# The product with w_out as seven products of halves, on a hybrid decoder block in fp32

## The chip, the cores and the metric

The kernel runs on one core of a Trainium2 chip. The metric is the device time of one execution in microseconds, as the median of several runs. Before the change it is 1438.05 us (three runs, 1435.02 to 1439.66).

## What is computed

One decoder block on 1024 tokens of width 1024, all in float32. The change concerns the second line from the end of the mixer and the layer norm behind it:

```python
proj = x @ w_in                       # q | f | i | og | pool_v | gate_a | gate_b
a = HGRN2(q, f, i) -> per-head RMSNorm * sigmoid(og) -> @ w_a
b = per-group linear(causal_mean_w(pool_v) - pool_v) * pool_scale
merged = sigmoid(gate_a) * a + sigmoid(gate_b) * b
x = layer_norm(alpha * x + merged @ w_out, ln1_g, ln1_b)
x = layer_norm(alpha * x + relu(x @ w_up)^2 @ w_down, ln2_g, ln2_b)
```

w_out is 1024 x 1024, w_up 1024 x 4096.

## The kernel before, in words

**Precision.** TensorE multiplies in a rounded fp32 form, so each operand is split into a high part (a copy in that form, on ScalarE) and a low part (operand minus high part, on VectorE). A product of two operands is three matmuls: high by high, high by low and low by high (mm3, L110 to L116).

**Seven products.** The products with w_in, w_a, w_up and w_down are computed with halves of tokens, of the contraction and of the columns by seven products instead of eight, with sums of halves made on VectorE ahead of them. The product with w_out is not: `mix(t, cc)` computes token tile t (128 tokens) by column half cc (512 columns) as 8 x 3 matmuls of 128x512 into one bank of PSUM. VectorE adds it to alpha times the row of x (L1390), takes statistics (L1332), and after the second half comes the layer norm of the row: aggregate (L1338), square root on ScalarE (L1339), normalising on ScalarE (L1350), times gamma on VectorE (L1351), plus beta on GpSimd (L1352). The rows 6 and 7 use two passes on VectorE instead (L1343, L1346), in halves of the row.

**Stages.** `a_pair(p)` makes two 128-row blocks of a, transposed (width by tokens), by seven products. `gated` loads the gate and the pooled branch from DRAM, multiplies and adds on VectorE (L1269, L1270) and gets a tile of merged: 128 of the width by 512 tokens. In before each is split at once (`split_act`, L121 and L122), or, for the first two pairs, kept in a pool and split later (`unpark`). The list `then` says what is recorded behind each of the seven steps of the last two pairs: there the rows of the first column half of w_out are loaded and split (`out_row`, L1253 and L1254). Then all `mix` calls are recorded: both halves of tiles 0 to 3, the transposes of these tokens for the MLP (`first_tokens`), and tiles 4 to 7.

**What sets the order.** The program is recorded in the order of the code, and a list scheduler with priorities (`tc.high_priority(PRIO)`) places each engine's instructions. Each engine then works its own queue strictly in order, and an instruction that waits holds up all behind it. Loads go out on SP, in its order, as soon as the buffer is free. `act_tile` gives an operand tile of two halves of 512 (high and low), `c_tile` and `block_tile` other 128x512 buffers, and `w_tile` the parts of a weight. The PSUM tags are "pj" (4 banks), and "hg", "sc" and "tr".

Of the kernel before, what the change touches and what calls it, by code (L numbers as in the profile page):

```python
# [13 lines left out]
ALU = mybir.AluOpType  # L14
# [38 lines left out]
def tile_hybrid_block(  # L53
# [119 lines left out]
    def transposed(tiles, off, kp, tag):  # L173

        ps = ps_tile(tag, 2)
        for c in range(CH):
            done = PE.transpose(ps[:, c * P : (c + 1) * P], tiles[c][:, off + kp * P : off + (kp + 1) * P], ident)
        return ps, done.ins
# [577 lines left out]
    with tc.tile_pool(name="tmp", bufs=1, side="right", reuse_waits="tile") as tmp:  # L756
# [492 lines left out]
        pk, parked, wo = [], {}, []  # L1249

        def out_row(raw, tile_of):
            hi, lo = tile_of()
            A.copy(hi, raw)  # L1253
            V.tensor_sub(lo, raw, f(hi))  # L1254
            wo.append((hi, lo))

        def parts_of(tile_of):
            def two():
                t = tile_of()
                return t[:, 0], t[:, 1]  # L1260
            return two

        def gated(j, u, park):

            def take(src):
                with tc.issue_after(last_load[0]):
                    t = loaded(gad[j][u], mg_tile("ga", 10))
# [3 lines left out]
                if park:  # L1271
                    parked[u, j] = t
                else:
                    merged[u][j] = split_act(t)
# [14 lines left out]
        def unpark(*which):  # L1289
            for u, j in which:  # L1290
                merged[u][j] = split_act(parked[u, j])

        def out_rows_of(*ks):
            for k in ks:
                out_row(loaded(w_out[k * P : (k + 1) * P, :HALF], c_tile), parts_of(act_tile))
# [17 lines left out]
    with tc.tile_pool(name="pk", bufs=1, side="right", reuse_waits="tile") as parking:  # L1313
        pk.append(parking)
        for i in range(2, 7):
            step(i)
        two = [a_pair(p) for p in range(2, 4)]
        then = (
            lambda: unpark((0, 0), (0, 1), (0, 2), (0, 3)), lambda: out_rows_of(0, 1, 2, 3), lambda: out_rows_of(4, 5, 6, 7),
            lambda: None, lambda: None, lambda: None, lambda: None,  # L1320
        )
        for i, after in enumerate(then):
            run(*(p[i : i + 1] for p in two))
            after()
        unpark((1, 0), (1, 1), (1, 2), (1, 3))
# [41 lines left out]
    xt[0] = [c_tile() for _ in range(CH)]  # L1367
    with tc.tile_pool(name="wo", bufs=1, side="right", reuse_waits="tile") as mp:
        st1 = [None] * 8
        g1, b1 = ln_params(lambda: f(act_tile()).rearrange("p a b -> p (a b)"), ln1_g, ln1_b)  # L1370
        for k2 in range(0, KT, 2):
            raw = raw_rows(w_out, k2, 1)
            for k in range(2):
                n = len(wo)
                out_row(raw[k], (
                    (lambda: (row_tile(), row_tile())) if n < 10 else
                    parts_of(act_tile if n < 12 else lambda: mp.tile([P, 2, HALF], F32R, tag="wo", name=nm("wo"), bufs=4))
                ))

        def mix(t, cc):  # L1380
            u, c = divmod(t, CH)
            if cc == 0:
# [7 lines left out]
            V.scalar_tensor_tensor(rc, rc, ALPHA, ps, ALU.mult, ALU.add)  # L1390
            stats(r[t], cc, st1[t])
            if cc == 1:
# [5 lines left out]
        for cc in range(2):  # L1398
            for t in range(CH):
                mix(t, cc)  # L1400
# [286 lines left out]
```

## Time and profile before

| | before |
|---|---|
| median of three runs | 1438.05 us |
| the profiled execution | 1434.66 us, span 1433.0 us |
| granted clock of TensorE | 0.999 |
| busy: TensorE, VectorE, ScalarE, GpSimd | 99%, 77%, 53%, 8% of the span |
| first w_out matmul, first MLP product | 710.3 us, 811.9 us |
| last w_a products | up to about 727 us, between the first w_out ones |

In the profile, PE is TensorE, DVE VectorE, ACT ScalarE and POOL GpSimd; PEld are the loads of the stationary operand. A row of a group gives the line, the engine, the operation, the tiles written and read, the shape, the count, then busy time and the mean ns of one, then the idle time before it and what ended that. A row of a timeline gives start, duration, engine, line, operation and tiles. Consecutive instructions of one engine overlap a little, so that they start closer together than they last.

### The profile page before, as it was taken

The page shows a single profiled execution, that of the slowest core. Times are in us where ns is not written, and L with a number is a line of the kernel's source. Part 1 is how long each engine was busy: PE and PEld are TensorE (multiplying, and loading weights), DVE is VectorE, ACT ScalarE, POOL GpSimd, SP SyncE. Part 2 cuts the span into 40 slices and gives each one's busy share as a digit, 9 for nine tenths or more (in the row PEclk, how much of TensorE's full clock was granted, in tenths as well). Part 3 has the DMA queues.
Part 4 walks back from the last instruction along what each step waited for, and adds up shares of the span by engine and source line. Part 5 has one row for each costly group of instructions (what it writes and reads, how often), then busy time and mean ns, then how long its engine had stood idle before and what let it go on. Part 6 is the DMA issues. An engine that isn't in the chain of part 4 may idle for free.

```text
span 1433.0 us, 21208 instructions
## 1 busy us (share of the span) xinstructions
PE 1420.8 (99%) x7499; PEld 1180.1 (82%) x7499; DVE 1099.2 (77%) x1832; ACT 753.2 (53%) x1376; POOL 110.9 (8%) x300
## 2 busy tenths in 40 slices
PE   9999999999999999999999999999999999999997
PEld 7888888888888888878888888888888888888886
DVE  6967887897797796679965697666666887777978
ACT  5445566566656656455522376555556433433534
POOL 0002011111212110100003000000000100000000
PEclk9999999999999999999999999999999999999999
DMA  7142254444444546899551315444457864444422
GB/s 272 60 140 89 90 131 148 126 115 150 113 118 133 150 123 190 237 322 340 182 198 74 103 59 188 153 159 161 162 177 243 299 235 146 150 151 157 132 74 118
DMA packets 187179, 228.18 MB, mean 159 GB/s; under 512 B 12576, under 2 KB 111168, under 8 KB 187072
## 3 DMA queue, kind: packets, MB, share of 16 engines
q1 hardware_dynamic: 180464, 210.94, 44.6%
q0 software_dynamic: 5824, 13.63, 4.7%
q10 hardware_dynamic: 784, 2.25, 0.5%
q8 instruction: 59, 0.97, 0.3%
q14 instruction: 48, 0.39, 0.1%
HBM read 149.70 MB, written 77.07 MB: 158 GB/s over the span
## 4 chain that ended last, share of the span: by engine, by line
PE 95%; DVE 2%; DMA 1%; ACT 1%; issue 1%; POOL 0%; DVEq 0%; ACTq 0%; SPq 0%; POOLq 0%
PE ps_pj L219 16%; PE ps_pj L222 16%; PE ps_pj L221 16%; PE ps_pj L1565 4%; PE ps_pj L1566 4%; PE ps_pj L1564 4%; PE ps_pj L115 2%; PE ps_pj L114 2%; PE ps_pj L116 2%; PE ps_tr L1566 2%; PE ps_tr L1565 2%; PE ps_tr L1564 2%; PE ps_hg L219 1%; PE ps_sc L219 1%; PE ps_sc L222 1%; PE ps_hg L221 1%
## 5 line engine op out<-in xcount | busy, mean ns | idle before, releaser
L219 PE MATMUL ps_pj<-act,w 128*128 128x512 f32 x1068 | 419.9, 393 | 0.3 <-ACT c L303 0.2
L222 PE MATMUL ps_pj<-act,w 128*128 128x512 f32 x1068 | 415.3, 390 | 0.0
L221 PE MATMUL ps_pj<-act,w 128*128 128x512 f32 x1068 | 415.3, 389 | 0.0
L256 ACT CAST w<-raw 128x512 fp32r<-128x512 f32 x303 | 187.7, 621 | 255.4 <-PE ps_pj L221 169.7
L257 DVE TENSOR_TENSOR w<-raw,w 128x512 fp32r<-128x512 f32 x303 | 207.2, 686 | 93.6 <-ACT w L256 92.3
L219 PEld LDWEIGHTS ps_pj<-act,w 128*128 128x128 f32 x1068 | 200.5, 188 | 44.1 <-ACT c L303 1.3
L222 PEld LDWEIGHTS ps_pj<-act,w 128*128 128x128 f32 x1068 | 200.5, 188 | 42.4
L221 PEld LDWEIGHTS ps_pj<-act,w 128*128 128x128 f32 x1068 | 200.6, 188 | 40.5
L1526 ACT CAST act<-act 128x1024 fp32r<-128x1024 f32 x66 | 67.0, 1050 | 108.2 <-issue 35.0
L1527 DVE TENSOR_TENSOR act<-act,act 128x1024 fp32r<-128x1024 f32 x66 | 79.4, 1220 | 18.1 <-ACT act L1526 18.1
L1566 PE MATMUL ps_pj<-act,act 128*128 128x512 f32 x240 | 93.0, 389 | 0.0
L1565 PE MATMUL ps_pj<-act,act 128*128 128x512 f32 x240 | 93.0, 389 | 0.0
L1564 PE MATMUL ps_pj<-act,act 128*128 128x512 f32 x240 | 92.5, 389 | 0.0
L307 DVE TENSOR_TENSOR c<-c,ps_pj 128x512 f32<-128x512 f32 x91 | 62.1, 682 | 32.5 <-PE ps_pj L222 31.8
L303 ACT COPY c<-ps_pj 128x512 f32<-128x512 f32 x92 | 53.3, 581 | 3.0 <-PE ps_pj L222 1.9
L1564 PEld LDWEIGHTS ps_pj<-act,act 128*128 128x128 f32 x240 | 45.0, 188 | 9.4
L1565 PEld LDWEIGHTS ps_pj<-act,act 128*128 128x128 f32 x240 | 45.0, 188 | 9.4
L1566 PEld LDWEIGHTS ps_pj<-act,act 128*128 128x128 f32 x240 | 45.0, 188 | 9.3
L312 DVE TENSOR_TENSOR raw<-raw,raw 128x512 f32<-128x512 f32 x43 | 29.6, 689 | 25.5 <-DMA raw<-in_w_in_dram 16.1
L1435 ACT ACTIVATE c<-c 128x512 f32<-128x512 f32 x61 | 38.5, 632 | 1.7
L1434 ACT ACTIVATE c<-c 128x512 f32<-128x512 f32 x46 | 29.0, 632 | 16.4 <-DVE c L307 16.4
L751 POOL DMA_DIRECT2D s<-og x28 | 24.9, 1161 | 133.2 <-DVE og L1177 133.2
(433 smaller groups left out, 2684.6 us busy)
## 6 DMA issues: line engine op xcount, KB each, us to landing
h<-c SPq DMA_DIRECT2D x106, 256.0 KB, 3.0
raw<-in_w_in_dram SPq DMA_DIRECT2D x100, 256.0 KB, 3.3
act<-h SPq DMA_DIRECT2D x78, 256.0 KB, 3.0
draw<-in_w_down_dram SPq DMA_DIRECT2D x16, 1024.0 KB, 8.2
raw<-in_w_up_dram SPq DMA_DIRECT2D x56, 256.0 KB, 2.9
hf<-h SPq DMA_DIRECT2D x34, 256.0 KB, 3.0
s<-og POOLq DMA_DIRECT2D x28, 256.0 KB, 6.4
v<-v SPq DMA_DIRECT2D x16, 256.0 KB, 3.5
```

The costliest lines, as they stand in the source:

```text
L219: PE.matmul(ps, wh[:, k], th, start=first and k == 0, stop=False, skip_group_check=True)
L221: PE.matmul(ps, wh[:, k], tl, start=False, stop=False, skip_group_check=True)
L222: PE.matmul(ps, wl[:, k], th, start=False, stop=k == CH - 1, skip_group_check=True)
L256: hi_of.append(A.copy(hi, src).ins)
L257: lo_of.append(V.tensor_sub(lo, src, f(hi)).ins)
L303: noted(A.copy(t, ps))
L307: last_add[0] = V.tensor_add(t, t, ps).ins
L1526: A.copy(hi, src)
L1527: V.tensor_sub(lo, src, f(hi))
L1564: PE.matmul(ps, hh[:, w], wh, start=fresh and n == 0, stop=False, skip_group_check=True)
L1565: PE.matmul(ps, hh[:, w], wl, start=False, stop=False, skip_group_check=True)
L1566: PE.matmul(ps, hl[:, w], wh, start=False, stop=n == M - 1, skip_group_check=True)
```

## The change

Tokens are halved into u = 0 (tiles 0 to 3) and u = 1, the contraction and the columns of w_out into halves as well. With A11, A12 the two halves of merged of the first tokens, A21, A22 those of the second, and B11, B12, B21, B22 the quarters of w_out, the products are p1 = A11 B11, p2 = A12 B21, p3 = S4 B22, p4 = A22 T4, p5 = S1 T1, p6 = S2 T2, p7 = S3 T3. The sums of tokens are S3 = A11 - A21 (GpSimd), S2 = A22 - S3, S1 = S2 + A11 and S4 = A12 - S2 (VectorE); those of rows are T3 = B22 - B12, T1 = B12 - B11, T2 = T3 + B11 and T4 = B21 - T2 (GpSimd). Each product is 4 token tiles by 4 row blocks by 3 terms. p6, p5 and p3 accumulate in the banks of p1, p4 in those of p7, which p2 had before; every stage of these sums is added to its row of x at once on VectorE (L1417, L1419 in the changed kernel), 28 evictions in all. On TensorE the scheduler puts the products in the order p1, half of p2's contraction, p6, p5, the rest of p2, p3, p7, transposes, p4, transposes.

The high parts of all rows and sums of rows are cast on ScalarE (L1292), their low parts made on GpSimd (L1293). The parking of gated tiles goes: those of the last two pairs are loaded into halves of operand tiles (`half_act`) and are split where they are used. The rows of tokens 0 to 3 are finished by p3, and their layer norm follows each; the transposes `first_tokens` come between p7 and p4; rows 4 to 7 are finished by p4. Layer norm itself is the same code (L1371, L1374, L1379 and L1380 are the changed kernel's lines for L1343, L1346, L1351 and L1352 of before).

```diff
-        ps = ps_tile(tag, 2)
+        ps = ps_tile(tag, 4 if tag == "pj" else 2)
...
-        pk, parked, wo = [], {}, []
-
-        def out_row(raw, tile_of):
-            hi, lo = tile_of()
-            A.copy(hi, raw)
-            V.tensor_sub(lo, raw, f(hi))
-            wo.append((hi, lo))
-
-        def parts_of(tile_of):
-            def two():
-                t = tile_of()
-                return t[:, 0], t[:, 1]
-            return two
+        pk, free_halves = [], []
+
+        def half_act():
+            if not free_halves:
+                t = f(act_tile())
+                free_halves.extend((t[:, 0], t[:, 1]))
+            return free_halves.pop(0)
...
-                    t = loaded(gad[j][u], mg_tile("ga", 10))
+                    t = merged[u][j] = loaded(gad[j][u], mg_tile("ga", 8) if park else half_act)
...
+        def split_rows(srcs, tile_of):
+            made = []
+            for t in srcs:
+                hi, lo = tile_of()
+                A.copy(hi, t)
+                G.tensor_sub(lo, t, f(hi))
+                made.append((hi, lo))
...
+        def split_a11():
+            out_ops["p1"] = [split_tokens(tokens(0, 0))]
+            for k in range(CH):
+                G.tensor_sub(merged[1][k], merged[0][k], merged[1][k])
+
+        def split_b11():
+            b_rows["b11"] = out_rows(0, 0, c_tile)
+            out_ops["p1"].append(split_rows(b_rows["b11"], act_parts))
+
+        def make_t3_t1():
+            b12, b22 = b_rows["t1"], b_rows["t3"] = [out_rows(kh, 1, half_act) for kh in range(2)]
+            for k in range(CH):
+                G.tensor_sub(b22[k], b22[k], b12[k])
+                G.tensor_sub(b12[k], b12[k], b_rows["b11"][k])
+
+        def make_t2():
+            b_rows["t2"] = b_rows["b11"]
+            for t, t3 in zip(b_rows["t2"], b_rows["t3"]):
+                G.tensor_add(t, t3, t)
+
+        def split_t2():
+            out_ops["p6"] = [split_rows(b_rows["t2"], act_parts)]
...
+    then = split_a11, lambda: None, split_b11, make_t3_t1, make_t2, split_t2, lambda: None
...
-            ps = ps_tile()
-            w = slice(c * P, (c + 1) * P)
-            mm3(ps, [(merged[u][k][0][:, w], merged[u][k][1][:, w], *wo[cc * KT + k]) for k in (0, 1, 2, 3, 4, 6, 5, 7)])
-            rc = r[t][:, cc * HALF : (cc + 1) * HALF]
-            V.scalar_tensor_tensor(rc, rc, ALPHA, ps, ALU.mult, ALU.add)
-            stats(r[t], cc, st1[t])
...
-        for cc in range(2):
-            for t in range(CH):
-                mix(t, cc)
...
+    chains = [[ps_tile(tag, 2) for tag in ("hg", "hg", "tr", "tr")], [ps_tile() for _ in range(CH)]]
...
+            for k, ((xh, xl), (wh, wl)) in enumerate(zip(xs, ws)):
+                PE.matmul(ps, xh[:, w], wh, start=fresh and k == 0, stop=False, skip_group_check=True)
+                PE.matmul(ps, xh[:, w], wl, start=False, stop=False, skip_group_check=True)
+                PE.matmul(ps, xl[:, w], wh, start=False, stop=k == CH - 1, skip_group_check=True)
+            y = r[t][:, nh * HALF : (nh + 1) * HALF]
+            with tc.high_priority(PRIO):
+                if (t, nh) in begun:
+                    V.tensor_add(y, y, ps)
+                else:
+                    V.scalar_tensor_tensor(y, y, ALPHA, ps, ALU.mult, ALU.add)
+                    begun.add((t, nh))
+                if whole:
+                    stats(r[t], nh, st1[t])
+            if then:
+                then(t)
...
+    s2 = [half_act() for _ in range(CH)]
+    for k in range(CH):
+        V.tensor_sub(s2[k], merged[1][CH + k], merged[1][k])
+    out_ops["p6"].insert(0, split_tokens(s2))
+    r = [None] * 8
+    out_product("p1", 1, True, 0, 0, False)
+    for k in range(CH):
+        V.tensor_add(merged[0][k], s2[k], merged[0][k])
+    out_ops["p5"] = split_tokens(tokens(0, 0)), split_rows(b_rows["t1"], row_parts)
+    out_product("p6", 1, False, 1, 0, False)
+    b21 = out_rows(1, 0, raw_row)
+    out_ops["p2"] = split_tokens(tokens(0, 1)), split_rows(b21, act_parts)
+    t4 = [half_act() for _ in range(CH)]
+    for t, row, t2 in zip(t4, b21, b_rows["t2"]):
+        G.tensor_sub(t, row, t2)
+    out_product("p5", 1, False, 1, 1, False)
+    for k in range(CH):
+        V.tensor_sub(merged[0][CH + k], merged[0][CH + k], s2[k])
+    out_ops["p3"] = split_tokens(tokens(0, 1)), split_rows(out_rows(1, 1, c_tile), row_parts)
+    out_product("p2", 0, True, 0, 0, True)
+    out_ops["p7"] = split_tokens(tokens(1, 0)), split_rows(b_rows["t3"], act_parts)
+    out_product("p3", 1, False, 0, 1, True, norm_row)
+    out_ops["p4"] = split_tokens(tokens(1, 1)), split_rows(t4, act_parts)
+    out_product("p7", 0, True, 1, 1, True)
+    xt[:] = [r[c][:, HALF:] for c in range(CH)], [c_tile() for _ in range(CH)], [r[c][:, :HALF] for c in range(CH)]
+    first_tokens("a12", "pj")
+    first_tokens("a11", "pj")
+    out_product("p4", 0, False, 1, 0, True, norm_row)
```

Three places of the order. The first is GpSimd around the end of the w_a products. Before, behind the last loads of o, it has nothing but the adds of beta:

```order
L735 DMA c_1373_7244<-o6_0_940 128x512
L735 DMA c_1375_7249<-o7_0_942 128x512
L1352 TENSOR_TENSOR r_1593_8246<-r_1593_8246,act_1574_8202 128x1024
L1352 TENSOR_TENSOR r_1596_8276<-r_1596_8276,act_1574_8202 128x1024
L1352 TENSOR_TENSOR r_1599_8306<-r_1599_8306,act_1574_8202 128x1024
L1352 TENSOR_TENSOR r_1602_8336<-r_1602_8336,act_1574_8202 128x1024
```

In the changed kernel the loads of o are followed by the sums T3 (L1318), T1 (L1319), T2 (L1324) and low parts of rows (L1293); c_1510 to c_1513 hold the rows of B11 and then T2, act_1522 and act_1523 B12 and then T1, act_1524 and act_1525 B22 and then T3; here its last part:

```order
L1319 TENSOR_TENSOR act_1523_7876<-act_1523_7876,c_1512_7821 128x512
L1293 TENSOR_TENSOR w_1582_8283<-act_1522_7873,w_1581_8282 128x512
L1318 TENSOR_TENSOR act_1525_7882<-act_1525_7882,act_1523_7876 128x512
L1293 TENSOR_TENSOR act_1542_7993<-c_1510_7817,act_1542_7993 128x512
L1293 TENSOR_TENSOR act_1543_7996<-c_1511_7819,act_1543_7996 128x512
L1324 TENSOR_TENSOR c_1512_7821<-act_1525_7882,c_1512_7821 128x512
L1293 TENSOR_TENSOR w_1584_8287<-act_1522_7873,w_1583_8286 128x512
L1319 TENSOR_TENSOR act_1523_7876<-act_1523_7876,c_1513_7823 128x512
L1293 TENSOR_TENSOR w_1586_8291<-act_1523_7876,w_1585_8290 128x512
L1293 TENSOR_TENSOR act_1544_7999<-c_1512_7821,act_1544_7999 128x512
L1324 TENSOR_TENSOR c_1513_7823<-act_1525_7882,c_1513_7823 128x512
L1293 TENSOR_TENSOR w_1588_8295<-act_1523_7876,w_1587_8294 128x512
```

Forty-eight instructions of 128x512 have come ahead of the adds of beta; the last T2 is the L1324 into c_1513_7823, the last row but one here.

The second place is where the last w_a product leaves its bank, which p1's last token tile takes over. ScalarE in the changed kernel: L1292 are casts of rows of w_out (c_1512 and c_1513 are T2, c_1615 is a row of B22), L121 casts of S2 (act_1563, act_1564) and of A11:

```order
L1292 CAST w_1585_8290<-act_1523_7876 128x512
L1292 CAST act_1544_7999<-c_1512_7821 128x512
L1292 CAST w_1587_8294<-act_1523_7876 128x512
L1292 CAST w_1619_8476<-c_1615_8468 128x512
L1292 CAST act_1545_8002<-c_1513_7823 128x512
L1389 DMA act_1553_8172<-in_ln1_g_dram 128x1024
L1389 DMA act_1554_8174<-in_ln1_b_dram 128x1024
L121 CAST act_1565_8190<-act_1563_8184 128x512
L121 CAST act_1566_8193<-act_1563_8184 128x512
L121 CAST act_1567_8196<-act_1564_8185 128x512
L121 CAST act_1568_8199<-act_1564_8185 128x512
```

The casts of S2 stand behind those of T2. VectorE in the changed kernel, S1's sums (L1446), the low parts of S2 (L122) and the last gated tile (L1263 reads the bank, L1264 adds the pooled branch):

```order
L1446 TENSOR_TENSOR ga_1469_7638<-act_1563_8184,ga_1469_7638 128x512
L122 TENSOR_TENSOR act_1565_8190<-act_1563_8184,act_1565_8190 128x512
L1446 TENSOR_TENSOR ga_1416_7416<-act_1564_8185,ga_1416_7416 128x512
L122 TENSOR_TENSOR act_1566_8193<-act_1563_8184,act_1566_8193 128x512
L1446 TENSOR_TENSOR ga_1471_7656<-act_1564_8185,ga_1471_7656 128x512
L122 TENSOR_TENSOR act_1567_8196<-act_1564_8185,act_1567_8196 128x512
L1263 TENSOR_TENSOR act_1550_8025<-act_1550_8025,ps_pj_1486_7698 128x512
L122 TENSOR_TENSOR act_1568_8199<-act_1564_8185,act_1568_8199 128x512
L1264 TENSOR_TENSOR act_1550_8025<-act_1550_8025,gb_1551_8027 128x512
```

and in before, with the same gated tile at L1269 and L1270:

```order
L1269 TENSOR_TENSOR ga_1559_8026<-ga_1559_8026,ps_pj_1484_7683 128x512
L1270 TENSOR_TENSOR ga_1559_8026<-ga_1559_8026,gb_1560_8028 128x512
L122 TENSOR_TENSOR act_1561_8032<-ga_1559_8026,act_1561_8032 128x512
L1269 TENSOR_TENSOR ga_1562_8047<-ga_1562_8047,ps_pj_1486_7698 128x512
L1270 TENSOR_TENSOR ga_1562_8047<-ga_1562_8047,gb_1563_8049 128x512
L122 TENSOR_TENSOR act_1564_8053<-ga_1562_8047,act_1564_8053 128x512
L122 TENSOR_TENSOR act_1565_8056<-ga_1444_7523,act_1565_8056 128x512
L122 TENSOR_TENSOR act_1566_8059<-ga_1461_7593,act_1566_8059 128x512
L122 TENSOR_TENSOR act_1567_8062<-ga_1447_7544,act_1567_8062 128x512
```

Before, the eviction (L1269 from ps_pj_1486_7698) stands behind the low parts of the tiles just ahead of it; in the change it stands behind three low parts of S2, whose casts come behind T2's.

The third place is the end of the product on VectorE. In the changed kernel (r_8298 to r_8346 are rows 4 to 7, L133 low parts of the transposes of the first tokens):

```order
L1417 TENSOR_TENSOR r_8330<-r_8330,ps_tr_8178 128x512
L1376 RECIPROCAL lmv_8857<-lmv_8857 128x1
L1417 TENSOR_TENSOR r_8346<-r_8346,ps_tr_8179 128x512
L1360 BN_STATS lst_8331<-r_8330 128x6
L1377 TENSOR_SCALAR lmv_8857<-lmv_8857 128x1
L1360 BN_STATS lst_8347<-r_8346 128x6
L133 TENSOR_TENSOR act_8789<-ps_pj_8784,act_8789 128x512
L1366 BN_AGGR lmv_8880<-lst_8331 128x2
L133 TENSOR_TENSOR act_8798<-ps_pj_8793,act_8798 128x512
L1366 BN_AGGR lmv_8903<-lst_8347 128x2
L133 TENSOR_TENSOR act_8807<-ps_pj_8802,act_8807 128x512
L1371 SCALAR_TENSOR_TENSOR r_8330<-r_8330,lmv_8880,act_8172 128x512 x2
```

In before, rows 6 and 7 (r_8714, r_8780):

```order
L1332 BN_STATS lst_8715<-r_8714 128x6
L1338 BN_AGGR lmv_8771<-lst_8715 128x2
L1343 SCALAR_TENSOR_TENSOR r_8714<-r_8714,lmv_8771,act_8200 128x512 x2
L1344 RECIPROCAL lmv_8771<-lmv_8771 128x1
L1346 SCALAR_TENSOR_TENSOR r_8714<-r_8714,lmv_8771,act_8202 128x512 x2
L1390 SCALAR_TENSOR_TENSOR r_8780<-r_8780,ps_pj_8783 128x512
L1332 BN_STATS lst_8781<-r_8780 128x6
L1390 SCALAR_TENSOR_TENSOR r_8780<-r_8780,ps_pj_8810 128x512
L1332 BN_STATS lst_8781<-r_8780 128x6
L1338 BN_AGGR lmv_8837<-lst_8781 128x2
L1343 SCALAR_TENSOR_TENSOR r_8780<-r_8780,lmv_8837,act_8200 128x512 x2
```

Before, row 6 has gone through its layer norm when row 7's first half is evicted; in the change the rows 6 and 7 are evicted one after the other, with row 5's layer norm and the transposes' low parts still in the queue.

More of the change, by code (lines that the diff above doesn't have):

```diff
@@ L1311, in tile_hybrid_block @@
             step(i)
[L1313 to L1325, printed above, removed]
+    pk_scope = ExitStack()
+    pk.append(pk_scope.enter_context(tc.tile_pool(name="pk", bufs=1, side="right", reuse_waits="tile")))
+    for i in range(2, 7):
+        step(i)
+    two = [a_pair(p) for p in range(2, 4)]
+    then = split_a11, lambda: None, split_b11, make_t3_t1, make_t2, split_t2, lambda: None
+    for i, after in enumerate(then):
+        run(*(p[i : i + 1] for p in two))
+        after()
     mg_scope.close()
@@ new lines, in raw_row, with row_parts @@
+    def raw_row():
+        return block_tile((HALF,))
+    def row_parts():
+        return row_tile(), row_tile()
+    s2 = [half_act() for _ in range(CH)]
[7 more added lines that the diff above has]
+    out_ops["p5"] = split_tokens(tokens(0, 0)), split_rows(b_rows["t1"], row_parts)
@@ L1409, in tile_hybrid_block @@
+    pk_scope.close()
     M = 4
```

64 lines of the change are left out of this document (28 added, 36 removed).

## The prediction

> **What bounds the kernel now.** I read the page first, for the busy shares and the chain that ended last, and then the waits of TensorE.
>
> ```profile
> PE 1420.8 (99%) x7499; PEld 1180.1 (82%) x7499; DVE 1099.2 (77%) x1832; ACT 753.2 (53%) x1376; POOL 110.9 (8%) x300
> PE 95%; DVE 2%; DMA 1%; ACT 1%; issue 1%; POOL 0%; DVEq 0%; ACTq 0%; SPq 0%; POOLq 0%
> PE ps_hg L480 <- POOL ident masks.py:199: 1.8, 1, 1.8
> PE ps_tr L114 <- DVE f L905: 1.4, 1, 1.4
> ```
>
> TensorE is busy for 99% of the span, the chain is TensorE for 95% of it, and its two longest waits are 1.8 and 1.4 us. A matmul that is taken away is therefore worth its whole slot, as long as nothing new makes TensorE wait. How much room the other engines have around the product with w_out is in the view by stretches of 20 us, and the slot of a matmul is in the timeline of TensorE.
>
> ```profile
> 680.00:700.00 20.00, 20.00 (x90) 16.57 (x89) 19.54 (x33) 11.48 (x21) 0.00 (x0) 1.00 0.55 170
> 700.00:720.00 20.00, 20.00 (x90) 16.57 (x89) 18.54 (x31) 8.46 (x16) 0.00 (x0) 1.00 0.58 177
> 720.00:740.00 20.00, 20.00 (x90) 16.53 (x90) 15.82 (x26) 7.08 (x13) 0.00 (x0) 1.00 0.69 254
> 740.00:760.00 20.00, 20.00 (x90) 16.57 (x89) 9.92 (x18) 5.50 (x7) 2.74 (x2) 1.00 0.36 112
> 760.00:780.00 20.00, 20.00 (x94) 16.40 (x93) 10.13 (x21) 4.79 (x8) 6.84 (x3) 1.00 0.19 79
> 800.00:820.00 20.00, 20.00 (x101) 16.92 (x100) 14.73 (x26) 5.82 (x12) 0.00 (x0) 1.00 0.32 107
> 840.00:860.00 20.00, 19.78 (x87) 16.03 (x87) 20.00 (x34) 14.77 (x27) 0.00 (x0) 1.00 0.16 53
> ```
> ```profile
> 710.30 0.39 PE L114 MATMUL ps_pj<-act,act 128*128 128x512 f32 x1
> ...
> 710.98 0.39 PE L114 MATMUL ps_pj<-act,act 128*128 128x512 f32 x1
> ...
> 785.66 1.03 PE L177 MATMUL ps_tr<-ident,r 128*128 128x128 f32 x8
> ```
>
> The columns are PE, weight loads, DVE, ACT and POOL busy, then the granted clock (1.00). VectorE is nearly full up to 720 us (19.54 and 18.54 of 20), half idle from 740 to 780, and full again at 840 to 860, where TensorE has its only small hole. GpSimd does nothing before 740. Three matmuls take 0.68 us, so one takes 0.227 us; eight transposes take 1.03 us, of which the last one's own duration is about 0.27, so one takes about 0.11 us.
>
> **What goes.** The product has 8 token tiles by 2 halves by 24 matmuls, 384; seven products of 4 tiles by 4 rows of w_out by 3 terms by 4 are 336. 48 x 0.227 = **-10.9 us** on TensorE.
>
> **What is added elsewhere.** Durations are from the groups by form between 600 and 880 us, and the spacing of queued VectorE instructions from its timeline.
>
> ```profile
> L122 DVE TENSOR_TENSOR act<-ga,act 128x512 fp32r<-128x512 f32 x16 | 10.7, 688 | 2.8 <-ACT act L121 2.7
> L121 ACT CAST act<-ga 128x512 fp32r<-128x512 f32 x16 | 9.4, 620 | 17.4 <-DVE ga L1270 17.4
> L1390 DVE SCALAR_TENSOR_TENSOR r<-r,ps_pj 128x512 f32<-128x512 f32 x16 | 10.9, 684 | 15.6 <-PE ps_pj L116 14.9 <-DMA r<-in_x_dram 0.7
> L1352 POOL TENSOR_TENSOR r<-r,act 128x1024 f32<-128x1024 f32 x6 | 14.4, 2399 | 149.0 <-DVE r L1351 137.2 <-PE ps_tr L177 9.3 <-DMA x<-r 2.5
> ```
> ```profile
> 692.82 0.69 DVE L257 TENSOR_TENSOR w<-raw,w 128x512 fp32r<-128x512 f32 x1
> 693.42 0.69 DVE L1270 TENSOR_TENSOR ga<-ga,gb 128x512 f32<-128x512 f32 x1
> 694.02 0.68 DVE L307 TENSOR_TENSOR room<-room,ps_pj 128x512 f32<-128x512 f32 x1
> ```
>
> A VectorE instruction on 128x512 starts every 0.60 us. VectorE gets 12 more evictions (28 for 16), 12 more low parts of tokens (28 for 16) and 12 sums, and loses the 16 low parts of w_out: +20, about 12 us. ScalarE gets 24 more casts, 24 x 0.62 = 15 us in a stage where it is at most 11.5 of 20 busy; I charge nothing for them by themselves: they lie in its idle time, and where one stands in a chain it is in the waits below. The gated tiles are now loaded into halves of operand tiles that TensorE frees late; the first such load goes out at 694.4 (70 matmuls ahead of the 710.3 mark) and so lands some 3 us after the place of its first use in before. VectorE has lost four low parts of w_out right behind it, 2.4 us, and I charge 0; without that cover it is 3 us. GpSimd gets 28 low parts and 20 sums, 48 instructions of 128x512. Its only large operation before is the six adds of 2.40 us for 128x1024. Half of it is 1.20 us; with a fixed part as large as a whole small operation (0.2 us, below) it would be 1.30. I take 1.20, so 48 are 58 us where there was nothing.
>
> **What the path sees of it: the first wait.** In the order of the changed kernel, p1's last token tile needs the bank that the last w_a product leaves. Its eviction (L1263 into act_1550_8025 from ps_pj, shown with the change) stands on VectorE behind the low parts of S2, their casts stand on ScalarE behind the casts of T2 (L1292), and the last of those waits for the last sum on GpSimd (L1324). So GpSimd's sums now reach TensorE. p1's last tile starts 84 matmuls after the place of the first w_out product: 710.3 + 84 x 0.227 = 729.4.
>
> Queues alone: the 18 GpSimd instructions from the first T3 to the last T2 can begin when b22 has come. Its buffers are freed 49 matmuls ahead of the 710.3 mark, at 699.2; six loads stand ahead of it on SP.
>
> ```profile
> 698.35 1.02 SPq L723 DMA_DIRECT2D c<-in_w_out_dram  x2
> ...
> raw<-in_w_in_dram SPq DMA_DIRECT2D x100, 256.0 KB, 3.3
> ```
>
> Six loads at 0.5 us and its own 3.3 make 705.5, some 706 with the wait for the buffer. 706 + 18 x 1.20 = 727.6; then one cast, and about 5 us of casts, low parts and evictions: 733.5, **4 us late**, and 2 to 3 us more where p2's rows b21 are cast and split behind it. 6.5 us in all.
>
> **A second price: VectorE and GpSimd get in each other's way.** The trace of before shows it at GpSimd's small operations.
>
> ```profile
> L1038 POOL TENSOR_TENSOR dec<-p x16: 190/198/776, 125.9 to 518.1; 128x4 f32<-128x4 f32 x16
> ```
> ```profile
> 164.90 0.68 POOL L1038 TENSOR_TENSOR dec<-p 128x4 f32<-128x4 f32 x1
> 165.52 0.18 POOL L1042 COPY eq<-p 128x4 f32<-128x4 f32 x1
> ...
> 514.95 1.49 POOL L1029 COPY T<-tA 128x32 f32<-128x32 f32 x1 [0.95 <-DVE tA L1014]
> ```
> ```profile
> 164.84 0.68 DVE L1050 TENSOR_TENSOR q<-q,tA 128x512 f32<-128x512 f32 x1
> 165.44 0.74 DVE L1116 COPY_PREDICATED att<-cmask,sc 128x512 f32<-128x512 uint32 x1
> ...
> 515.38 0.43 DVE L931 TENSOR_TENSOR pC<-pA 128x269 f32<-128x269 f32 x1
> 515.73 0.68 DVE L1018 TENSOR_TENSOR_SCAN tC<-f,starts 128x255 f32<-128x255 f32 x1
> ```
>
> L1038 has a median of 0.198 us. At 164.90 it took 0.68: VectorE had begun L1050, with two inputs in SBUF, at 164.84, and L1038 ended when that did. The next small one, beside an instruction that also reads a PSUM score, took 0.18. At 514.95 a copy of 128x32 took 1.49 us and ended with VectorE's second instruction in a row. So GpSimd stands still while VectorE reads two tiles of SBUF. The other direction, VectorE behind a long GpSimd operation, the trace cannot show: the six adds of 2.40 us met only VectorE instructions with a PSUM input, statistics and small ones.
>
> The Trainium skill, "SBUF — State Buffer", section "Who interferes with whom", says that a VectorE instruction with two SBUF inputs and a GpSimd instruction that reads SBUF exclude each other for a whole instruction, whichever starts first. The rows above agree for the one direction, and no row of before shows the other. By that rule the change pays the sum of the two queues instead of the longer one; without it, the queues alone.
>
> I take the two queues as one where both read SBUF. From the moment that L1264 ends the last gated tile of the first half of tokens (L1270 in before, 693.42, so 694.1), the rows up to p1's last bank are 23 of GpSimd and 32 of VectorE with two SBUF inputs: 23 x 1.20 + 32 x 0.60 = 46.8 us, 740.9, against the 729.4 that TensorE wants: **11.5 us late** in place of 4. On to the last low part for p3 (L1293 of c) there are 19 of GpSimd and 29 of VectorE, 22.8 + 17.4 = 40.2: 781.1, against 710.3 + 252 x 0.227 = 767.5: **13.6 us late**. That is no second stall of its size but 2 us more. The lower end is the 6.5 us of the queues alone, as if GpSimd held nobody up; the upper one 17, with 3 us more for casts and low parts that come behind the sums. The rows of GpSimd's small operations lie at the upper side: **+14**.
>
> **The end of the product.** In before the row of a token tile is finished every 24 matmuls or later; in the changed kernel rows 4 to 7 are all finished inside p4, one every 12 matmuls, 2.7 us. Their layer norms crowd together.
>
> ```profile
> L1332 DVE BATCH_NORM_STATS2 lst<-r 128x6 f32<-128x512 f32 x16 | 11.0, 692 | 0.4
> L1351 DVE TENSOR_TENSOR r<-r,act 128x1024 f32<-128x1024 f32 x6 | 7.4, 1226 | 7.0 <-ACT r L1350 7.0
> L133 DVE TENSOR_TENSOR act<-ps_tr,act 128x512 fp32r<-128x512 f32 x12 | 8.0, 685 | 8.1 <-ACT act L132 8.0
> L1343 DVE SCALAR_TENSOR_TENSOR r<-r,lmv,act 128x512 f32<-128x512 f32 x4 | 2.8, 750 | 0.1
> ```
>
> From the eviction of p4's second tile to the last step of row 7 VectorE has 15 instructions at 0.60 (evictions, statistics, low parts, one weight), 2 at 1.15, 8 halves of rows at 0.67 and small ones of about 1: 17.7 us. TensorE has 48 matmuls and 32 transposes until it needs that row: 10.9 + 3.5 = 14.4. **+3.3 us**; beside GpSimd's 2.40 us add of row 5 it could be 5.5. I take 4. From the first MLP product on, VectorE was full already (20.00 of 20) and only 1 us of TensorE was lost there; a later start lets the weights of the MLP be split ahead, and I charge 0.
>
> **Sum.** -10.9 + 14 + 4 = **+7 us**. The profiled execution took 1434.66 us (span 1433.0), so 1441.7; the median of the three runs, 1438.05, stands 3.4 above it, so the forecast is **1445.0**.
>
> **Rivals.**
> 1. *No contention that counts, the queues alone.* For it: in before no VectorE instruction is ever seen longer beside GpSimd. Against: GpSimd itself is held up, and it is the late one here. -10.9 + 6.5 + 3.3 = -1: 1437.
> 2. *GpSimd is in time* (faster). Its place is the wait of p1's last tile. If a 128x512 operation costs 1.0 us or less, 18 of them end at 724, the 5 us behind them fit before 729.4, and nothing is late until the layer norms: -10.9 + 3.3 = -7.6: 1430.5. For it speaks only that VectorE falls to 9.9 of 20 after 740 and so could hold nobody up; against it stands 2.40 us for twice the size.
> 3. *GpSimd starves.* As at 514.95, VectorE keeps the port through several instructions in a row, and as VectorE is nearly full to 720, GpSimd gets only the gaps: its 23 operations start to move after 720, 720 + 23 x 1.20 + 5 = 753, 23 late. -10.9 + 23 + 5.5 = +18: 1456.
> 4. *The change doesn't save its matmuls.* The order of the changed kernel has the 48 fewer; this gets no chance.
>
> **Chances.** Forecast 0.60, first rival 0.17, second 0.18, third 0.05. About 0.3% (4.3 us) is what a measurement of this kernel can tell from no change. The forecast's lateness of 6.5 to 17 and its end of 3.3 to 5.5 give -1 to +12, of which I put a fifth, 0.12, within 0.3%; the first rival falls there whole. Faster 0.18, same 0.12 + 0.17 = 0.29, slower 0.48 + 0.05 = 0.53. The forecast's own range is 1437 to 1450. The second rival alone holds nearly 2 in 10, so the whole range reaches to it and to the third: 1430 to 1456.
>
> **What would show it.** Right: TensorE waits of some 10 us in all between 725 and 770, at p1's last tile and at p2's first rows, ended by the last eviction of w_a, by casts and by GpSimd; GpSimd's 128x512 operations longer than 1.2 us where VectorE is full, or VectorE spaced wider than 0.60 there; then some 3 to 5 us of waits for the layer norms of rows 5 to 7. Wrong: no TensorE wait before 770 (second rival), GpSimd operations of 1.2 us all along with waits of 4 and 2 us (first), or a stretch without GpSimd progress up to 720 (third). A first MLP product before 806 would mean that the early waits are not there at all.

## The result, and the profile after

The changed kernel takes 1458.67 us (median of four runs, 1456.46 to 1460.53) against 1437.61 us of the kernel before beside it: a ratio of 1.0147, with a 95% interval of 1.0125 to 1.0169. That is 21 us more, where +7 was forecast, and above the end of the range (1456). The direction was right and the mechanism is there to be seen; the size was three times the forecast.

The page first: busy shares and the chain that ended last, and below them the waits of TensorE (in us, number, longest).

```profile
PE 1419.3 (97%) x7451; PEld 1173.9 (80%) x7451; DVE 1139.7 (78%) x1852; ACT 765.9 (53%) x1400; POOL 188.2 (13%) x348
PE 85%; DVE 5%; DMA 3%; issue 3%; ACT 1%; POOL 1%; SPq 0%; DVEq 0%; ACTq 0%; POOLq 0%
```
```profile
PE ps_pj L1411 <- DVE act L1263: 13.2, 2, 8.5
PE ps_pj L219 <- ACT r L194: 2.6, 1, 2.6
PE ps_hg L1412 <- POOL act L1293: 1.8, 1, 1.8
...
PE ps_pj L221 <- DVE act L133: 1.5, 1, 1.5
PE ps_pj L219 <- DVE c L307: 1.4, 1, 1.4
```

TensorE has 48 matmuls fewer, yet its share of the chain fell from 95% to 85%. The largest wait is the one that was named: the eviction L1263 that frees p1's banks, 13.2 us in two waits. Where this is in the program, the stretches of 20 us show (PE, weight loads, VectorE, ScalarE, GpSimd busy, then the granted clock).

```profile
700.00:720.00 20.00, 20.00 (x90) 16.49 (x88) 12.69 (x16) 7.74 (x16) 11.42 (x9) 1.00 0.73 240
720.00:740.00 20.00, 12.10 (x50) 8.78 (x48) 19.76 (x16) 4.26 (x8) 20.00 (x13) 0.97 0.41 129
740.00:760.00 20.00, 10.91 (x28) 7.72 (x28) 17.16 (x24) 9.28 (x17) 11.01 (x7) 0.69 0.58 199
820.00:840.00 20.00, 15.67 (x82) 12.49 (x80) 19.44 (x36) 12.79 (x25) 5.92 (x3) 1.00 0.24 92
860.00:880.00 20.00, 17.98 (x77) 13.89 (x76) 20.00 (x34) 12.83 (x24) 0.00 (x0) 1.00 0.11 33
```

Look at the counts beside the busy times. From 720 to 740 VectorE is busy for 19.76 us with 16 instructions; in before the same stretch had 26 in 15.82. GpSimd is busy for all of it with 13. The timelines of the two engines show why, first GpSimd, then VectorE:

```profile
734.14 1.72 POOL L1324 TENSOR_TENSOR c<-act,c 128x512 f32<-128x512 f32 x1
735.81 1.72 POOL L1293 TENSOR_TENSOR w<-act,w 128x512 fp32r<-128x512 f32 x1
```
```profile
727.99 1.67 DVE L1264 TENSOR_TENSOR act<-act,gb 128x512 f32<-128x512 f32 x1
729.58 0.67 DVE L307 TENSOR_TENSOR room<-room,ps_pj 128x512 f32<-128x512 f32 x1
...
732.97 6.78 DVE L1441 TENSOR_TENSOR act<-act,ga 128x512 f32<-128x512 f32 x4
```

L1264 and L1441 read two tiles of SBUF and take 1.7 us each in place of 0.68; L307, with one input in PSUM, takes 0.67 between them. GpSimd's operations take 1.72. The two engines take turns, one instruction each. The other direction, which the trace of before could not show, is here: VectorE waits for GpSimd too. The Trainium skill, "SBUF — State Buffer", section "Who interferes with whom", states this exclusion for whole instructions, and the 1.7 us of both agree with it.

At TensorE the two waits cost more than their length:

```profile
742.07 0.80 PE L1411 MATMUL ps_pj<-act,act 128*128 128x512 f32 x1 [8.50 <-DVE act L1263]
742.66 0.63 PE L1412 MATMUL ps_pj<-act,act 128*128 128x512 f32 x1
743.09 0.63 PE L1413 MATMUL ps_pj<-act,act 128*128 128x512 f32 x1
...
745.88 0.40 PE L1411 MATMUL ps_pj<-act,act 128*128 128x512 f32 x1
746.11 0.39 PE L1412 MATMUL ps_pj<-act,act 128*128 128x512 f32 x1
```

After the wait a matmul takes 0.43 us instead of 0.23, for some eight of them, and then the old pace is back. The clock of 0.69 in the stretch from 740 to 760 is the same thing.

**Where the time went.** I took the starts of TensorE's matmuls one after another and summed what is over 0.227 us (0.109 for a transpose) by more than 0.15. Between 700 and 790 us that is 22.4 us: 2.0 at the last w_a products, 13.5 at p1's banks, 3.9 of matmuls at half clock behind those two waits, 3.0 at p2's first rows. Between 790 and 850 it is 5.7 us (0.4 in before), between 850 and 900 2.5 (nothing in before). 22.4 + 5.3 + 2.5 - 10.9 = 19.3 of the 21 us by the runs. The rest lies in delays of 0.15 us or less in the same stretches: summed without that threshold the three are 23.1, 5.6 and 3.0 us more than in before, and the sum is 20.8.

The profiled execution itself is 25.8 us longer in its span, and part of that arises long before the change, where the code and the order of the two kernels are the same. VectorE stands still there, first in before, then in the changed kernel:

```profile
478.87 0.69 DVE L312 TENSOR_TENSOR raw<-raw,raw 128x512 f32<-128x512 f32 x1 [3.04 <-issue]
```
```profile
483.42 0.69 DVE L312 TENSOR_TENSOR raw<-raw,raw 128x512 f32<-128x512 f32 x1 [7.08 <-issue]
```

The view names no releaser ("issue"), but the trace has one. VectorE waits for a 256 KB load of w_in, which SP issued at 473.57 us in before and which landed at 478.79; in the changed kernel it was issued at 474.07 and landed at 483.34. In both VectorE starts 0.08 us behind the landing. What TensorE loses between 478 and 500 goes with the time of this load:

| runs | time of the load, us | TensorE loses, us |
|---|---|---|
| before | 5.2 | 0.2 |
| e1, e2, e3, e4, e6, e7, e9, e11 | 6.5 to 7.4 | 1.2 to 2.0 |
| the change, e5, e8, e10, e12 | 8.3 to 9.3 | 3.3 to 4.4 |

In the last five the granted clock also fell to half for 3.4 us there. No edit touches this load, and before has only one profile, so it is not shown that the change makes it slower; why its time differs is open. It is 4.2 of the 5 us by which the profiled execution's 25.8 us exceed the 20.8; how much of it is in the medians is not known.

### The profile page after: what moved, and what is told of

It is laid out like the page before. It is cut to its first block, busy times and chain, and to the rows that moved or that the text cites. A ratio compares the mean times of both kernels' runs of the same rounds, so it can differ in the third digit from the quotient of the medians.

```text
span 1458.8 us, 21242 instructions
## 1 busy us (share of the span) xinstructions
PE 1419.3 (97%) x7451; PEld 1173.9 (80%) x7451; DVE 1139.7 (78%) x1852; ACT 765.9 (53%) x1400; POOL 188.2 (13%) x348
## 4 chain that ended last, share of the span: by engine, by line
PE 85%; DVE 5%; DMA 3%; issue 3%; ACT 1%; POOL 1%; SPq 0%; DVEq 0%; ACTq 0%; POOLq 0%
PE ps_pj L219 15%; PE ps_pj L221 15%; PE ps_pj L222 15%; PE ps_pj L1626 4%; PE ps_pj L1627 4%; PE ps_pj L1625 4%; PE ps_tr L1625 1%; PE ps_tr L1627 1%; PE ps_tr L1626 1%; PE ps_hg L222 1%; PE ps_sc L221 1%; PE ps_sc L219 1%; PE ps_hg L221 1%; PE ps_hg L219 1%; PE ps_sc L222 1%
## 5 line engine op out<-in xcount | busy, mean ns | idle before, releaser
L257 DVE TENSOR_TENSOR w<-raw,w 128x512 fp32r<-128x512 f32 x303 | 213.3, 707 | 91.9 <-ACT w L256 89.9
L307 DVE TENSOR_TENSOR c<-c,ps_pj 128x512 f32<-128x512 f32 x91 | 62.1, 682 | 35.5 <-PE ps_pj L222 35.0
L312 DVE TENSOR_TENSOR raw<-raw,raw 128x512 f32<-128x512 f32 x43 | 29.6, 689 | 28.5 <-DMA raw<-in_w_in_dram 18.5
L1635 POOL DMA_DIRECT2D act<-x x7 | 3.7, 532 | 313.0 <-DVE act L1588 307.1
L751 POOL DMA_DIRECT2D s<-og x28 | 24.9, 1161 | 133.4 <-DVE og L1177 133.4
L1495 ACT ACTIVATE c<-c 128x512 f32<-128x512 f32 x46 | 29.1, 633 | 20.4 <-DVE c L307 20.4
```

Of the source, the lines that this page charges most:

```text
L257: lo_of.append(V.tensor_sub(lo, src, f(hi)).ins)
L307: last_add[0] = V.tensor_add(t, t, ps).ins
```

## The experiments

The sums for TensorE are formed in each as above: "early" is 700 to 790 us, "end" 790 to 850, "MLP" 850 to 900. The change has 22.4, 5.7 and 2.5, at +21 us. Differences in us are the ratio's part times 1437.

| run | ratio, 95% interval | early | end | MLP |
|---|---|---|---|---|
| the change | 1.0147, 1.0125 to 1.0169 | 22.4 | 5.7 | 2.5 |
| e1, all 48 on VectorE | 1.0069, 1.0054 to 1.0085 | 10.9 | 6.7 | 2.5 |
| e2, more gb buffers | 1.0170, 1.0155 to 1.0185 | 23.7 | 5.7 | 2.5 |
| e3, GpSimd only writes | 1.0040, 1.0027 to 1.0053 | 3.7 | 6.2 | 4.0 |
| e4, S2 split later | 1.0168, 1.0150 to 1.0187 | 23.1 | 5.8 | 2.5 |
| e5, loads on GpSimd | 1.0156, 1.0137 to 1.0176 | 25.1 | 5.8 | 2.5 |
| e6, p7 and p4 in turn | 1.0178, 1.0155 to 1.0201 | 24.9 | 8.7 | 3.1 |
| e7, e1 and e6 | 1.0061, 1.0038 to 1.0085 | 10.5 | 5.4 | 2.5 |
| e8, 28 low parts on VectorE | 1.0110, 1.0087 to 1.0134 | 18.5 | 4.2 | 3.7 |
| e9, no loads for T3, T1 | 1.0147, 1.0129 to 1.0165 | 21.2 | 9.1 | 2.1 |
| e10, GpSimd writes three times | 1.0014, 1.0004 to 1.0023 | 2.3 | 5.8 | 3.7 |
| e11, 20 sums on VectorE | 1.0105, 1.0088 to 1.0122 | 16.2 | 4.3 | 3.9 |
| e12, no norm of rows 4 to 7 | 1.0116, 1.0087 to 1.0146 | 23.9 | 0.2 | 1.1 |

Two theories stood for the early part. **Port**: VectorE and GpSimd pay the sum of their queues. **Load**: in the trace GpSimd stood for 7.7 us until B12 and B22 had come, and SP had waited for VectorE with the loads ahead of them.

**e1.** GpSimd's 48 operations on VectorE (G to V in L1293, L1309, L1318, L1319, L1324 and L1453):

```diff
-                G.tensor_sub(lo, t, f(hi))
+                V.tensor_sub(lo, t, f(hi))
...
```

> All 48 sums and low parts of 128x512 that the change put on GpSimd are put on VectorE, nothing else. Port theory (VectorE and GpSimd pay the sum of their queues, 1.7 us per pair, and that is most of the 22 us that TensorE loses between 720 and 760): each of the 48 then costs 0.6 us instead of 1.7, VectorE's two-input instructions are back at 0.68 us, and TensorE loses about 8 us there instead of 22: about 1445 us. Load theory (what is late is the loads of the gated tiles and of B12 and B22, which stand on SP behind gb loads that wait for VectorE): the chain of sums begins as late as before, and the time stays above 1453 us.

Measured: +10 us, the early part 10.9. VectorE does all of it and yet gets there sooner. From 708 to 755 us its timeline runs in steps of 0.60, with two stands of about 0.5 us for loads of gates:

```profile
719.50 0.69 DVE L1324 TENSOR_TENSOR c<-act,c 128x512 f32<-128x512 f32 x1
720.11 0.69 DVE L1293 TENSOR_TENSOR act<-c,act 128x512 fp32r<-128x512 f32 x1
720.71 0.68 DVE L307 TENSOR_TENSOR room<-room,ps_pj 128x512 f32<-128x512 f32 x1
```

As the port theory said; the load theory's 1453 or more is out. Of the 10.9 that are left, 3.0 are matmuls at half clock. The longest waits are 4.0 us for the eviction L1263 in VectorE's full queue and 3.2 for a cast of p2's rows, which stands on ScalarE behind casts that had waited for VectorE.

**e2.** More buffers for the loads ahead on SP:

```diff
-                    more = loaded(pbd[j][u], mg_tile("gb", 2))
+                    more = loaded(pbd[j][u], mg_tile("gb", 4))
...
-            room = mg_tile("room", 6)
+            room = mg_tile("room", 4)
```

> The buffers of the pooled branch (gb) go from 2 to 4, so that its loads don't hold up SP; the buffers of room go from 6 to 4 to make place. Load theory: the first T3 on GpSimd starts about 8 us earlier relative to TensorE, and the time falls by 8 us or more, to 1450 or below. Port theory: the chain starts earlier but runs into a fuller VectorE; at most 4 us are won, 1455 to 1459 us.

Measured: +24 us. But the first T3 starts 0.8 us after p1's first matmul, where it was 0.9 in the change: the gb loads only ran further ahead and SP stood at the later ones. The edit did not do what it was made for, so it decides nothing.

**e3.** Fills in place of GpSimd's sums and low parts; what they should hold is left out:

```diff
-                G.tensor_sub(lo, t, f(hi))
+                G.memset(f(lo), 0.0)
...
```

> GpSimd's 48 sums and low parts become fills with zero of the same tiles: the instruction reads nothing of SBUF, so these operands are wrong, but the tiles, the loads and the order remain. Port theory: VectorE's two-input instructions stay at 0.60 us apart beside GpSimd, and TensorE loses 8 us or less between 720 and 760: 1445 us or below. Load theory: the fills of B12 and B22 still wait for their loads, and the time stays above 1452 us.

Measured: +6 us, the early part 3.7. It fits the port theory, but a fill takes 0.47 us where a sum takes 1.27 to 1.31 undisturbed, so GpSimd's own queue was shorter as well. e10 was made for that.

**e4.** The split of S2 recorded behind p1:

```diff
-    out_ops["p6"].insert(0, split_tokens(s2))
     r = [None] * 8
     out_product("p1", 1, True, 0, 0, False)
+    out_ops["p6"].insert(0, split_tokens(s2))
```

> The split of S2 is recorded behind p1 instead of ahead of it, so that the eviction that frees p1's last bank needn't stand behind S2's low parts. Queue theory (the two waits of 8.5 and 4.7 us come from this place in VectorE's order): they go, and the time falls by 8 us or more, to 1450. Port theory and load theory: p6 waits instead for the same sums, within 4 us of the change, 1455 to 1460 us.

Measured: +24 us. The eviction still stands behind three low parts of S2 in VectorE's timeline: the scheduler put them there again, so this run decides nothing. But in e10 below the last eviction stands behind the low parts of S2 too, and TensorE waits only 0.3 us there. So this order alone does not make the wait.

**e5.** The loads of B12 and B22 on GpSimd's queue:

```diff
-            b12, b22 = b_rows["t1"], b_rows["t3"] = [out_rows(kh, 1, half_act) for kh in range(2)]
+            b12, b22 = b_rows["t1"], b_rows["t3"] = [out_rows(kh, 1, half_act, nc.gpsimd) for kh in range(2)]
...
```

> The eight loads of B12 and B22 are issued on GpSimd's queue, just ahead of the sums that need them, instead of on SP behind loads that wait for VectorE. The change stood at 1.0147 of the kernel before, +21 us. Load theory: the first T3, which began 15 us after GpSimd's last free moment, begins some 4 us earlier, and so does all behind it: about +17 us over the kernel before. Port theory (GpSimd and VectorE pay the sum of their two-input instructions until p1's last bank is free): the earlier start only moves the same work into a time in which VectorE has more to do, +19 to +22 us.

Measured: +22 us, but the first T3 at 1.3 us after p1's first matmul: eight loads issued on GpSimd, 0.55 us each, took the time that SP's queue had cost. Again no clean test, which led to e9.

**e9.** T3 and T1 from rows that are there, without the eight loads:

```diff
-            b12, b22 = b_rows["t1"], b_rows["t3"] = [out_rows(kh, 1, half_act) for kh in range(2)]
+            b12, b22 = b_rows["t1"], b_rows["t3"] = [[half_act() for _ in range(CH)] for kh in range(2)]
+            b11 = b_rows["b11"]
             for k in range(CH):
-                G.tensor_sub(b22[k], b22[k], b12[k])
-                G.tensor_sub(b12[k], b12[k], b_rows["b11"][k])
+                G.tensor_sub(b22[k], b11[k], b11[k])
+                G.tensor_sub(b12[k], b22[k], b11[k])
```

> B12 and B22 aren't loaded: T3 and T1 are formed from the rows of B11, which are there, so that these operands are wrong, while GpSimd's 48 operations, their buffers and VectorE's work remain; the eight loads go from SP. The change stands at +21 us. Load theory: the chain of sums starts some 8 us earlier and the time falls by 6 us or more, to +15 or below. Port theory: the chain then meets VectorE's two-input instructions earlier and both are slowed; 1 to 4 us are won, +17 to +20.

Measured: +21 us. Now the first T3 starts 9.4 us ahead of p1's first matmul, 10 us earlier than in the change, and the last bank is free 33.0 us after that matmul instead of 36.7 (TensorE wants it at 19.1). GpSimd, from the first T3 to the last low part of T1:

```profile
701.50 2.48 POOL L1319 TENSOR_TENSOR act<-c 128x512 f32<-128x512 f32 x2
703.95 3.45 POOL L1293 TENSOR_TENSOR act<-c,act 128x512 fp32r<-128x512 f32 x2
...
735.69 1.71 POOL L1293 TENSOR_TENSOR w<-act,w 128x512 fp32r<-128x512 f32 x1
```

Ten microseconds of head start gave 3.7 at the bank, 1.2 in the whole early part, and nothing in the time, which is a little above what either theory allowed. The chain met VectorE's instructions earlier and both were slowed. So the loads alone are not the cause; they are a part of it, 3.7 us at the bank.

**e10.** Each fill of e3 three times, so that GpSimd is busy as long as with sums:

```diff
-                G.memset(f(lo), 0.0)
+                G.memset(f(lo), 0.0)
+                G.memset(f(lo), 0.0)
+                G.memset(f(lo), 0.0)
...
```

> As in the run with fills in place of GpSimd's 48 operations, but each fill is made three times, 3 x 0.47 = 1.41 us in place of 1.25 us for an undisturbed sum: GpSimd is busy as long as with sums, and reads nothing of SBUF (operands are wrong). With one fill the kernel was at 1.004, +6 us, and TensorE lost 3.7 us between 700 and 790 us instead of 22.4. Port theory: within 2 us of that, since only what GpSimd reads counts. Queue theory (GpSimd's own 1.25 us per operation make its chain late, whether VectorE is disturbed or not): 8 us or more are lost there, +11 us or more.

Measured: +2 us, the early part 2.3, within 2 us of e3's as the port theory said. The time is 4 us better than e3's, which neither theory explains. Beside a GpSimd that is as busy, VectorE keeps its pace (first GpSimd's fills, then VectorE):

```profile
723.39 0.52 POOL L1294 MEMSET act<- 128x512 f32 x1
723.85 0.52 POOL L1293 MEMSET w<- 128x512 f32 x1
724.32 0.52 POOL L1324 MEMSET act<- 128x512 f32 x1
```
```profile
723.00 0.68 DVE L1451 TENSOR_TENSOR act<-act,ga 128x512 f32<-128x512 f32 x1
723.60 0.69 DVE L1456 TENSOR_TENSOR ga<-act,ga 128x512 f32<-128x512 f32 x1
724.20 0.68 DVE L307 TENSOR_TENSOR room<-room,ps_pj 128x512 f32<-128x512 f32 x1
```

These fills read no tile. So what costs 20 of the early 22.4 us is that GpSimd reads SBUF, and not how long it is busy. One reserve: a fill need not wait for the high part or for the tile it would subtract, so its chain is looser than that of the sums, and a part of the 20 can be that.

**e8 and e11.** A part of the 48 moved to VectorE: the 28 low parts (L1293), or the 20 sums (L1309, L1318, L1319, L1324, L1453).

> Only the 28 low parts go to VectorE; the 20 sums stay on GpSimd. Port theory, by the number of operations: 28 of 48 of the 11.5 us that the whole move brought, so about +14 us over the kernel before. Rival (what is late is GpSimd's own queue up to the last T2, in which 14 of the 23 operations are sums): only the sums' chain counts and it gets shorter by the low parts in it, so nearly the whole gain, +10 to +11 us.

> The counterpart of the run with the 28 low parts on VectorE (+16 us): here the 20 sums go to VectorE and the 28 low parts stay on GpSimd. Port theory, if each operation moved brings the same: 20 of 48 of 11.5 us, about +16 us. If the moves add up exactly, the two runs together bring the 11.5 us of the whole move: 5 there, so 6 to 7 here, +14 to +15. Queue theory: the sums' chain off GpSimd leaves the low parts alone there and brings nearly all, +11 us or less.

Measured: +16 and +15 us. The first brings 5.3 of the 21, the second 6.0, together 11.3, and the whole move of e1 brought 11.2. The parts add up, as a sum of two queues should, and the queue theory's +11 or less is out for both. Each of these differences is uncertain by some 4 us, by the intervals of the two ratios, so the adding up is not proved. Per operation a low part was worth 0.19 us and a sum 0.30, against 0.24 by count alone, which is not clear of this noise either.

**e6 and e7.** The tiles of p7 and p4 in turn, on the change and on e1:

```diff
...
-    out_product("p7", 0, True, 1, 1, True)
...
+    for p7, p4 in ((0, None), (1, 0), (2, 1)):
+        out_product("p7", 0, True, 1, 1, True, None, (p7,))
+        if p4 is not None:
+            out_product("p4", 0, False, 1, 0, True, norm_row, (p4,))
+    first_tokens("a12", "pj")
...
```

> The token tiles of p7 and p4 are taken in turn, with the transposes between them, so that rows 4 to 7 are finished further apart; nothing else changes. End theory (rows 4 to 7 finished inside p4 crowd their layer norms, 5.7 us of TensorE waits between 825 and 845): most of it goes, some 4 us less than the change, about +17 us over the kernel before. Rival (VectorE's work up to the MLP is the same and full, so the wait moves behind the first MLP products): within 1.5 us of the change, +20 to +22 us.

> The 48 operations on VectorE, and p7 and p4 in turn: both at once. With the first alone the kernel was 1.0069 of the kernel before, +9.6 us, of which 6.7 us of waits at the end of the product. If the terms add, about +5 us; if VectorE, full from 700 to 800 us, is the bound whatever the order, +8 to +10 us.

Measured: +26 and +9 us, no better than the kernels that they were made from; e6 is worse than both of its expectations, and its end lost 8.7 us, a part of it at half clock. Rows that finish further apart do not help, and a new wait, for an add of beta on GpSimd, came up:

```profile
PE ps_tr L177 <- POOL r L1380: 3.4, 1, 3.4
PE ps_pj L219 <- ACT r L194: 1.8, 1, 1.8
PE ps_pj L219 <- ACT c L303: 1.8, 1, 1.8
```

So either the layer norms' amount, not their place, sets the end, or it is not theirs at all. e12 tells these apart.

**e12.** The layer norms of rows 4 to 7 left out:

```diff
-        layer_norm(r[t], st1[t], g1, b1, 2 if t >= 6 else 0)
+        if t < CH:
+            layer_norm(r[t], st1[t], g1, b1, 0)
```

> The layer norms of rows 4 to 7 are left out (the MLP then works on rows that aren't normalised), about 9 us of VectorE's work with two GpSimd adds; all else is the change, which stands at +21 us. End theory (the layer norms crowd VectorE while TensorE goes through p4, the transposes and the first MLP products: 5.7 us of waits between 790 and 850 us and 2.5 between 850 and 900): both go but for 1 us, about +14 us. Rival (the first MLP product waits for ScalarE's copies of transposes and for banks, whatever VectorE has to do): at most 2 us are won, +19 or more.

Measured: +17 us with a wide interval (12.5 to 21), between the two expectations. The trace is clearer than the time: the end falls from 5.7 to 0.2 us and the MLP's part from 2.5 to 1.1. All the waits of TensorE between 780 and 900 us are now

```profile
PE ps_hg L219 <- ACT w L256: 0.5, 1, 0.5
PE ps_pj L219 <- ACT c L303: 0.3, 1, 0.3
```

The wait for ScalarE's copies (L194) went too, though no copy was taken away; in the change it stood behind a normalising pass (L1378) on ScalarE. The layer norms are the cause of what is lost at the end, and of 1.4 of the 2.5 us in the MLP.

## Why the prediction was wrong, step by step

- **What goes, -10.9 us**: right. TensorE has 7451 records for 7499, and e10, in which the rest nearly vanishes, stands at 2.3 + 5.8 + 3.7 - 0.4 - 10.9 = +0.5 by its trace and +2.0 by its runs.
- **The second price**: the mechanism was right, e1, e10, e8 and e11 show it. Its price was close: 1.20 + 0.60 = 1.80 a pair was forecast, and about 1.7 was measured, although an undisturbed GpSimd operation takes 1.27 to 1.31. The sum of the two queues from the last gated tile's end to p1's last bank was 46.8 us. In e9, without the loads of B12 and B22, it is 47.0: L1264 of that tile ends at 696.15 us and the eviction starts at 743.18. That this is so near is partly luck. 26 operations of GpSimd and 31 of VectorE fall in it, not 23 and 32, VectorE waits 1.7 us for a gate, and the last T2 ends at 727.3, so that the eviction waits for VectorE's own queue and not for T2 as the forecast had it. In the changed kernel the same stretch is 51.2 us. The rival without contention and the faster rival are out; GpSimd did not starve, it took turns.
- **The step that failed is "I take +14"**, the lateness of TensorE that was made of this sum: 22.4 was measured. Three parts were missing or small. The waits at p1's banks and at the last w_a products were 15.5 us for 11.5. A part of that is loads: VectorE stood 5.8 us until 719.7 for a gate's load into half of an operand tile, which I had charged at 0, and GpSimd 7.7 us until 715.6 for B12 and B22, and for 2.9 of the 51.2 us (0.6 in e9) neither had a two-input operation from SBUF running. p2's rows cost 3.0 for 2.1. And 3.9 us are matmuls at half clock behind the two long waits, for which there was no term at all.
- **The end, +4**: 5.3 more than before, the mechanism right (e12), the size near. The port was in it as forecast: two halves of row 7's first pass took 3.54 us beside the 2.83 us add of row 5, in place of about 1.4 and 2.4 (row 6's first pass, just ahead, took 1.40).

```profile
834.57 2.83 POOL L1380 TENSOR_TENSOR r<-r,act 128x1024 f32<-128x1024 f32 x1 [7.01 <-DVE r L1379]
```
```profile
834.41 3.54 DVE L1371 SCALAR_TENSOR_TENSOR r<-r,lmv,act 128x512 f32<-128x512 f32 x2
```

- **The MLP, 0**: 2.5. A later start did not let the weights be split ahead: VectorE was still busy for all of 860 to 880 us. The layer norms of rows 4 to 7 are 1.4 of it, which e12 gives back; the rest is open.
- **The range**: its upper end was the starving rival at +18. The terms that were missing belong to the forecast's own mechanism, and 17 us as the most for its wait left no room for a wait's after-effect.

No version here beats the kernel before: even with GpSimd's reads gone (e10) the change ends 0.6 to 3.3 us behind it. By e10's trace the 10.9 us saved are spent on 2.3 us early, 5.4 more at the end and 3.7 in the MLP. No run has both e10's fills and e12's missing layer norms, so what the two would give together is not shown.

## What to carry to other kernels

Here work that reads SBUF was not taken off VectorE by giving it to GpSimd: where both have two-input operations queued, count the sum of both queues, and compare it with the same work on VectorE alone (1.7 us a pair against 1.2). Where a forecast has a wait of TensorE of several microseconds, add what its clock loses behind it (about 2 us behind each of the two long ones here). And a load whose buffer now comes free later is to be priced with the queue that it blocks, even where it looks covered.

## What the runs showed of the hardware

TensorE's clock fell to half around a wait, in pieces of 3.4 us: the profile's clock records of the change show 6.8 us at half from 738.8 and from 749.0 us, at waits of 8.5 and 4.7 us, and those of e1 3.4 us from 733.1 and from 743.4, at waits of 4.0 and 3.2. A short wait may or may not bring it: the 2.6 us at the first MLP product left the clock at 1.00 in the change's profile and gave 3.4 us at half in e4's, and in e1 waits of 1.0, 1.8 and 1.0 close together gave 10.2 us from 815.1. The Trainium skill, "TensorE: Matmul & The Clock Gate", section "What's actually happening", gives a window of about 3.4 us of idling and a half rate until a window was busy. The lengths of the pieces agree with it, but the waits of 2.6 and 3.2 us that brought the half rate are shorter than that window.

Who goes first at SBUF: where the prediction's rows of before show a short GpSimd operation held up, it ended with VectorE's instruction, so that it looked as if only GpSimd gave way. With long operations on both sides neither starved in the changed kernel: each waited for one instruction of the other, at about 1.7 us a pair.
